# In every second weight chunk, a DMA adds the weights onto their negated high part to form the low part

## The chip, the cores and the metric

The kernel runs on one core of one Trainium2 chip. The metric is the device time of one execution in microseconds (us). Before the change the median of three runs is 1270.47 us (1269.8 to 1270.65).

## What is computed

The reference is a two-layer encoder over 256 tokens of width 2048, in fp32. Cut to what matters:

```python
# layer 0: differential attention (A) and spatial gating (B) from one input product
proj = rms_norm(x, g0) @ w_in            # 2048 x (4*2048 + 3*2048)
q, k, v, z_a, u_b, v_b, z_b = split(proj)
y_a = head_norm(diff_attention(q, k, v)) * silu(z_a)
y_b = spatial_gating(gelu(u_b), gelu(v_b)) * silu(z_b)
x = x + concat(y_a, y_b) @ w_out
# layer 1: a gated linear recurrence
xb, z_c = split(rms_norm(x, g1) @ w_in1)  # 2048 x (2*2688)
h = rg_lru(causal_conv4(xb))              # two block-diagonal gate products and a scan
x = x + (h * silu(z_c)) @ w_out1
return rms_norm(x, gf)
```

Nearly all the arithmetic is products of 256 tokens with some 229 MB of weights, each of which is used once.

## The kernel before

**Weights.** The weights are laid out in the order of their use as 228 chunks of up to 16 tiles of 128 x 128 (`plan()`): the chunks vb, u, zb, q, k, v, ob, za and oa of layer 0 (chunks 0 to 143), then the loop of layer 1 with its xb, zc and gt chunks (144 to 206), then the output product co (207 to 227). A full chunk is 128 x 2048 fp32, 1 MiB. The gate chunks gt are smaller, 4 to 8 tiles, and 21 of the 63 chunks of layer 1's loop are such.

**Products in parts.** The products run in a rounded fp32 format (F32R). To keep precision each operand is split into a high part (the value rounded to that format) and a low part (the rest, w minus its high part), and three of the four partial products are taken: high x high, high x low, low x high. So every chunk needs two SBUF tiles before TensorE can use it: `hi` and `lo`. `feat` (L264) and `tokn` (L280) hold the products; in each tile the product with `hi` comes first and the one with `lo` behind it.

**The walk.** `run` (L235) does one chunk per step. In step s TensorE does the products of chunk s, while the split of chunk s + 2 (`LA` = 2) and the load of chunk s + 5 (`LD` = 5) are recorded. `load` (L174) issues one DMA on SP's queue into a `raw` tile, of which there are three. `split_hi` (L192) is a ScalarE copy from `raw` to `hi`, `split_lo` (L207) a VectorE subtraction `lo = raw - hi`. `hi` and `lo` have three buffers each as well, so the buffer for chunk s + 2 is the one that chunk s - 1 used: the ScalarE copy of step s can start when TensorE is through with chunk s - 1, that is, at the moment when step s begins on TensorE. A `raw` buffer is free when the last reader of the chunk in it is through, and SP's DMA for the chunk three later waits for that. Chunks 0 to 5 (below `FINE` = 6) are loaded and split in quarters and aren't touched by the change.

**Order.** The order on each engine is written out by hand (`manual_schedule`): within a step come the work of phase -1 (evacuations of the products before), the split's ScalarE part, the work of phase 0, the split's VectorE part, the loads, the work of phase 1, the products, and the work of phase 2. All engines run their instructions in that order.

Of the kernel before, what the change touches and what calls it, by code (L numbers as in the profile page):

```python
# [11 lines left out]
AF = mybir.ActivationFunctionType  # L12
# [16 lines left out]
NEG = -3.0e38  # L29
# how far the recurrent branch's input product runs ahead of its gates  # L30
LEAD = 3
# the shift of the sigmoid that starts the reciprocal
SHIFT = 8.0

# columns of the packed per-feature parameters
PRM = {}
# [9 lines left out]
def gate_rows(j):  # L46
    """The 128-feature tiles that share a gate block with tile j."""
    heads = lambda t: set(range(t * P // CB, (t * P + P - 1) // CB + 1))
    return [k for k in range(KC) if heads(k) & heads(j)]


def z_rows(j):
    """The gate path's column tiles by the recurrent branch's tile j: at first the same, one behind later."""
    return range(j, j + 1) if j < KC // 2 else range(j - 1, j - (j == KC // 2))


def plan():
    """The weights' tiles in the order of their use: chunks of up to 16 tiles of 128 x 128."""
    chunks = []
    add = lambda kind, **kw: chunks.append(dict(kind=kind, **kw))  # L60
    for cb in range(4):
        for kq in range(4):
            add("vb", cb=cb, kq=kq, n=16)
    for ct in range(KD):
        add("u", ct=ct, n=16)
        add("zb", ct=ct, n=16)

    def heads(p):
        for h in (2 * p, 2 * p + 1):
            for j in range(2):  # L70
                add("q", h=h, j=j, n=16)
            for j in range(2):
                add("k", h=h, j=j, n=16)
        for kq in range(4):
            add("v", p=p, kq=kq, n=16)

    def za(p):
        for kq in range(4):
            add("za", p=p, kq=kq, n=16)

    def out(kind, rows, wait):
        """An output product; the first column tiles leave the row tiles from wait[1] on for later."""
        cols, late = wait
        order = [(f, k) for f in range(cols) for k in range(late)]
        order += [(f, k) for f in range(cols) for k in range(late, rows)]
        order += [(f, k) for f in range(cols, KD) for k in range(rows)]
        for t in range(0, len(order), 16):
            add(kind, fk=order[t:t + 16], n=len(order[t:t + 16]))

    heads(0)  # L90
    for f in range(KD):
        add("ob", f=f, n=16)
    za(0)
    for p in range(1, H // 2):
        heads(p)
        za(p)
    out("oa", KD, (4, KD - 4))
    for j in range(LEAD):
        add("xb", j=j, n=16)
    for j in range(KC):  # L100
        if j + LEAD < KC:
            add("xb", j=j + LEAD, n=16)
        for z in z_rows(j):
            add("zc", j=z, n=16)
        add("gt", j=j, n=2 * len(gate_rows(j)))
    add("zc", j=KC - 1, n=16)
    out("co", KC, (4, KD))
    off = 0
    for c in chunks:
        c["off"] = off  # L110
        off += c["n"] * P * P
    return chunks, off
# [3 lines left out]
def trunk(ctx, tc, xT, prm, rep, wsp, wst, out):  # L116
# [10 lines left out]

# [1 line left out]
    pt = cpool.tile([P, NPRM], F32, name="pt")  # L129
# [18 lines left out]

    # an operand's two parts lie side by side, tile by tile
    class Parts:  # L150
# [15 lines left out]

# [1 line left out]
    chunks, _ = plan()  # L168
# [5 lines left out]
    def load(c):  # L174
# [6 lines left out]
        for a in range(4):  # L181
# [3 lines left out]
            SP.dma_start(t[:, a * 512:a * 512 + 512], src[:, a * 512:a * 512 + 512])  # L185

    def split_x(k):
        A.activation(x.hi[k], res[:, k, :], AF.Copy, scale=par("g0", k))
        V.scalar_tensor_tensor(x.lo[k], res[:, k, :], par("g0", k), x.hi[k].bitcast(F32),
                               op0=ALU.mult, op1=ALU.subtract)  # L190

    def split_hi(c):  # L192
# [4 lines left out]
        if c >= FINE:  # L197
            A.copy(hi[:, :n], raw[c][:, :n])  # L198
            return
        for a in range(4):  # L200
# [6 lines left out]
    def split_lo(c):  # L207
        n = chunks[c]["n"] * P
        hi, lo = parts[c]
        if c >= FINE:  # L210
            V.tensor_sub(lo[:, :n], raw[c][:, :n], hi[:, :n].bitcast(F32))  # L211
        del raw[c]

    # the tensor engine's clock rises while the first loads are under way
    warm = pst.tile([P, 512], F32, tag="o", name="warm")
    for _ in range(10):
        T.matmul(warm[:, :P], ones, ones, start=True, stop=True)

# [1 line left out]
    def at(s, fn, ph=0):  # L220
        """Something due at step s: -1 before the coming chunk's first part, 0 and 1 before and after its second,
        2 after the products."""
        assert (s, ph) > passed[0], (s, ph)
        todo.setdefault((s, ph), []).append(fn)

    def due(s, ph):
        passed[0] = s, ph
        # what yields goes on by turns, so that an operation's wait for the one before it is used
        chains = [c for c in [fn() for fn in todo.pop((s, ph), [])] if isinstance(c, GeneratorType)]
# [5 lines left out]
    def run(emit):  # L235
        """One chunk: later ones' loads and splits, its products, and what is due."""
        s = pos[0]
# [24 lines left out]

# [1 line left out]
    def feat(ps, hi, lo, tiles, m, first, last, whole=False):  # L264
        """W.T x, feature by token, in two halves of ps that are yet to be added, or whole in the first:
        tiles = (tile of the chunk, row tile)."""
        for n, (w, k) in enumerate(tiles):
# [12 lines left out]
    def tokn(pss, hi, lo, kq, first, last):  # L280
        """pss[t][token, n] += x.T W, four row tiles of W, 512 columns."""
        for k in range(4):
# [11 lines left out]
    def halves(out, ps):  # L294
        """The sum of the two halves: ScalarE brings one, before the step's other work."""
        assert passed[0][1] == -1
# [5 lines left out]

# [1 line left out]
    def r_sum(more=()):  # L304
        """Per token 1 / rms, from the sums of squares in acc (and more)."""
        ps = pst.tile([P, 512], F32, tag="t", name="ps_r")
# [17 lines left out]
    def norm_at(s):  # L324
        """The norm's steps from s on; rb is there from step s + 3 on."""
        box = []
# [18 lines left out]

# [1 line left out]
    state = {}  # L347
# [7 lines left out]
    def token_chunks(name):  # L355
        """x.T W of the coming four chunks, 512 columns: a tile for each half of the tokens."""
        pss = [mm_tile(f"ps_{name}_{t}") for t in range(NT)]
# [8 lines left out]
    def do_heads(p):  # L366
        """The first two's tiles pass through pools that open only after step `start` where p is 0."""
        first = pos[0]
# [29 lines left out]

    # ======================= layer 0, the gated spans =======================
    with tc.tile_pool(name="pb", bufs=2) as pb:  # L400
# [7 lines left out]

        # the squares pass through the room of v
        sq = vx.rearrange("p t d -> p (t d)")  # L410
# [126 lines left out]

    # ======================= layer 0, attention =======================
    def lam_dots():
# [9 lines left out]
    def softplus():  # L549
        """4 softplus(-lambda) and -8 of it, softplus as max(-lambda, 0) + log1p(exp(-|lambda|)), log1p by 2 atanh(y / (2 + y))."""  # L550
        lam = par("lam", 0, KC)
# [17 lines left out]
    with tc.tile_pool(name="pa", bufs=2) as pa:  # L569
# [131 lines left out]

        # the gated spans' half of the output product stands in yh, yl until its last tile is through
        at(pos[0], lam_dots, 2)
# [7 lines left out]

# [1 line left out]
        def x1_add(f, ps):  # L713
# [8 lines left out]
        def out_product(kind, rows, done):  # L722
            """The chunks of an output product; done(f, ps, step) when a column tile is through."""
            cur = {}
# [20 lines left out]

    # ======================= layer 1 =======================
    with tc.tile_pool(name="pc", bufs=2) as pc:
# [45 lines left out]

        # with v = 4 softplus(-lambda) r: a = exp(-2 v) = q - 1, 1 - a^2 = tanh(v) q^2 and q = 2 / (1 + tanh(v)),
        # q by a Newton step from a sigmoid's tail
        def gates(j, ps):
# [101 lines left out]

# [1 line left out]
        last = []  # L900
# [22 lines left out]
def pack(np, i):  # L923
    """The inputs laid out as the program reads them."""
    w0, wo0, w1, wo1 = i["ab_w_in"][0], i["ab_w_out"][0], i["c_w_in"][0], i["c_w_out"][0]
# [84 lines left out]
```

## Time and profile before

| | |
|---|---|
| median of the runs | 1270.47 us |
| the profiled execution's own span | 1268.5 us |
| busy TensorE (PE) | 1256.2 us, 99% of the span |
| busy VectorE (DVE) | 837.2 us, 66% |
| busy ScalarE (ACT) | 641.4 us, 51% |
| busy GpSimd (POOL) | 81.7 us, 6% |
| DMA, mean over the span | 184 GB/s |

The profile is of one execution, whose span lies 2.0 us under the median. The rows below are of four kinds: the page's groups of instructions (count, busy time and mean of one), lists of waits (who waited for whom, total us, times, longest), time lines of one engine over a few steps, and tables of stretches with the busy time of each engine, the granted TensorE clock (1.00 is the full 2.4 GHz) and the share of time in which the 16 DMA engines were busy.

### The profile page before, as it was taken

To read this page: it belongs to the slowest core of one execution; us is meant where nothing else is said; L and a number is where in the kernel's file an instruction comes from. 1 tells how busy PE (TensorE), PEld (TensorE's weight loads), DVE (VectorE), ACT (ScalarE), POOL (GpSimd) and SP (SyncE) were. 2 spreads that over 40 slices of the span, in tenths; PEclk is the share of its full clock that TensorE was granted. 3 is DMA by queue.
4 is the path that set the end of the run, shared out by engine and by line. 5 is a ranking of instruction groups with operands and counts; after the bars stand their busy time and mean duration, and the time that the engine had idled before them with its cause. 6 is when DMAs were issued, how large, how long until landed. Compare 5 with 4: busy or idle time off the path is not lost.

```text
span 1268.5 us, 18568 instructions
## 1 busy us (share of the span) xinstructions
PE 1256.2 (99%) x7647; PEld 1122.2 (88%) x7647; DVE 837.2 (66%) x1116; ACT 641.4 (51%) x850; POOL 81.7 (6%) x72
## 2 busy tenths in 40 slices
PE   9999999999999999999999999999999999999996
PEld 7888888888888888888888888899999999998886
DVE  6747777776566547547547557667788888886543
ACT  7444444443353344444444344445767776685441
POOL 1100000000000000010010012330000000001331
PEclk9999999999999999999999999999999999999998
DMA  9654545455544554554454454544555555556541
GB/s 332 247 196 171 194 169 200 168 189 176 197 168 148 216 198 167 174 188 169 171 186 175 168 184 180 192 151 161 191 198 177 176 195 176 180 208 209 174 164 67
DMA packets 38533, 233.01 MB, mean 184 GB/s; under 512 B 4400, under 2 KB 5296, under 8 KB 12720
## 3 DMA queue, kind: packets, MB, share of 16 engines
q1 hardware_dynamic: 37296, 229.40, 51.3%
q10 hardware_dynamic: 1152, 2.42, 0.5%
q8 instruction: 60, 0.98, 0.3%
q14 instruction: 25, 0.20, 0.0%
HBM read 229.71 MB, written 2.10 MB: 183 GB/s over the span
## 4 chain that ended last, share of the span: by engine, by line
PE 96%; DVE 1%; issue 1%; DMA 1%; ACT 0%; SPq 0%; POOLq 0%; POOL 0%; DVEq 0%; ACTq 0%
PE ps_co L275 6%; PE ps_ob L275 5%; PE ps_k L275 5%; PE ps_q L275 5%; PE ps_zb L275 5%; PE ps_u L275 5%; PE ps_oa L275 4%; PE ps_xb L271 3%; PE ps_xb L273 3%; PE ps_xb L272 3%; PE ps_co L276 3%; PE ps_zc L273 3%; PE ps_zc L271 3%; PE ps_zc L272 3%; PE ps_u L276 2%; PE ps_q L276 2%
## 5 line engine op out<-in xcount | busy, mean ns | idle before, releaser
L211 DVE TENSOR_TENSOR lo<-raw,hi 128x2048 fp32r<-128x2048 f32 (+2 forms) x222 | 481.9, 2171 | 233.2 <-ACT hi L198 232.8
L198 ACT CAST hi<-raw 128x2048 fp32r<-128x2048 f32 (+2 forms) x222 | 402.4, 1813 | 356.5 <-PE ps_za L290 55.3
L275 PE MATMUL ps_co<-y,hi 128*128 128x512 f32 x315 | 110.2, 399 | 0.0
L273 PE MATMUL ps_zc<-x,lo 128*128 128x256 f32 x336 | 95.3, 284 | 0.2 <-DVE lo L211 0.2
L271 PE MATMUL ps_xb<-x,hi 128*128 128x256 f32 x336 | 95.4, 284 | 0.0
L273 PE MATMUL ps_xb<-x,lo 128*128 128x256 f32 x336 | 95.3, 284 | 0.0
L271 PE MATMUL ps_zc<-x,hi 128*128 128x256 f32 x336 | 95.2, 283 | 0.0
L272 PE MATMUL ps_zc<-x,hi 128*128 128x256 f32 x336 | 95.2, 283 | 0.0
L272 PE MATMUL ps_xb<-x,hi 128*128 128x256 f32 x336 | 95.2, 283 | 0.0
L275 PE MATMUL ps_zb<-x,hi 128*128 128x512 f32 x256 | 91.7, 399 | 0.0
L275 PE MATMUL ps_q<-x,hi 128*128 128x512 f32 x256 | 91.3, 399 | 0.0
L275 PE MATMUL ps_k<-x,hi 128*128 128x512 f32 x256 | 91.0, 399 | 0.0
L275 PE MATMUL ps_u<-x,hi 128*128 128x512 f32 x256 | 90.6, 393 | 0.0
L275 PE MATMUL ps_ob<-y,hi 128*128 128x512 f32 x256 | 90.5, 400 | 0.0
L276 PE MATMUL ps_co<-y,lo 128*128 128x256 f32 x315 | 86.0, 281 | 0.0
L275 PE MATMUL ps_oa<-y,hi 128*128 128x512 f32 x240 | 83.8, 399 | 0.0
L275 PEld LDWEIGHTS ps_co<-y,hi 128*128 128x128 f32 x315 | 58.4, 188 | 13.2
L276 PE MATMUL ps_q<-x,lo 128*128 128x256 f32 x256 | 69.2, 281 | 0.0
L276 PE MATMUL ps_ob<-y,lo 128*128 128x256 f32 x256 | 69.2, 281 | 0.0
L276 PE MATMUL ps_u<-x,lo 128*128 128x256 f32 x256 | 69.2, 281 | 0.0
L276 PE MATMUL ps_k<-x,lo 128*128 128x256 f32 x256 | 69.2, 280 | 0.0
L276 PE MATMUL ps_zb<-x,lo 128*128 128x256 f32 x256 | 68.5, 278 | 0.0
(288 smaller groups left out, 2854.6 us busy)
## 6 DMA issues: line engine op xcount, KB each, us to landing
raw<-in_wst SPq DMA_DIRECT2D x201, 1024.0 KB, 4.8
raw<-in_wst SPq DMA_DIRECT2D x26, 256.0 KB, 6.0
raw<-in_wst SPq DMA_DIRECT2D x11, 384.0 KB, 3.1
raw<-in_wst SPq DMA_DIRECT2D x8, 512.0 KB, 4.8
res<-in_xT SPq DMA_DIRECT2D x3, 512.0 KB, 7.2
out_x<-res SPq DMA_DIRECT2D x4, 256.0 KB, 2.3
out_x<-res ACTq DMA_DIRECT2D x3, 256.0 KB, 2.3
res<-in_xT SPq DMA_DIRECT2D x4, 128.0 KB, 3.5
```

The source lines that it names most:

```text
L198: A.copy(hi[:, :n], raw[c][:, :n])
L211: V.tensor_sub(lo[:, :n], raw[c][:, :n], hi[:, :n].bitcast(F32))
L271: T.matmul(ps[:, :S], hi[:, s], m.hi[k], start=a, stop=False)
L272: T.matmul(ps[:, :S], hi[:, s], m.lo[k], start=False, stop=False)
L273: T.matmul(ps[:, :S], lo[:, s], m.hi[k], start=False, stop=b)
L275: both = lambda: T.matmul(ps, hi[:, s], m.both[k], start=a, stop=b)
L276: small = lambda: T.matmul(ps[:, :S], lo[:, s], m.hi[k], start=False, stop=False)
```

## The change

In every chunk of even number from 6 on, the VectorE subtraction is gone. ScalarE writes the negated, rounded weights into `lo` right after it has written `hi`, and a DMA issued on GpSimd's queue then reads the chunk's weights from HBM again and adds them onto what stands in `lo`. Of the 222 chunks from 6 on these are 111. The chunk's own load into `raw` stays, since ScalarE reads it twice.

```diff
+    def by_dma(c):
+
+        return c >= FINE and c % 2 == 0
+
...
         if c >= FINE:
             A.copy(hi[:, :n], raw[c][:, :n])
+            if by_dma(c):
+                A.activation(lo[:, :n], raw[c][:, :n], AF.Copy, scale=-1.0)
+                src = wst[chunks[c]["off"]:chunks[c]["off"] + P * n].rearrange("(p c) -> p c", p=P)
+                GP.dma_start(lo[:, :n], src, accum_op=ALU.add)
             return
...
     def split_lo(c):
         n = chunks[c]["n"] * P
         hi, lo = parts[c]
-        if c >= FINE:
+        if c >= FINE and not by_dma(c):
             V.tensor_sub(lo[:, :n], raw[c][:, :n], hi[:, :n].bitcast(F32))
         del raw[c]
```

The rest of the diff takes out comments, so line numbers of the changed kernel differ by up to 8.

ScalarE's order in the ob chunks of layer 0, before (`hi`, `raw` and `lo` are a chunk's tiles, the numbers tell buffers apart, `l_y` is a small vector for layer 1):

```order
L198 CAST hi_3291<-raw_3167 128x2048
L554 ACTIVATE l_y<-pt 128x21
L555 ACTIVATE l_y<-l_y 128x21
L198 CAST hi_3356<-raw_3215 128x2048
L198 CAST hi_3397<-raw_3256 128x2048
L198 CAST hi_3438<-raw_3321 128x2048
```

And the same place in the changed kernel:

```order
L202 CAST hi_3323<-raw_3198 128x2048
L204 ACTIVATE lo_3324<-raw_3198 128x2048
L562 ACTIVATE l_y<-pt 128x21
L563 ACTIVATE l_y<-l_y 128x21
L202 CAST hi_3389<-raw_3247 128x2048
L202 CAST hi_3430<-raw_3288 128x2048
L204 ACTIVATE lo_3431<-raw_3288 128x2048
```

Every second copy into `hi` has an instruction that writes `lo` behind it, ahead of the step's other ScalarE work.

GpSimd's order from the start of layer 0 to its first attention heads, before (`rt`, `sd` and `ss` are the small vectors of the norms, raised to the power -1/2):

```order
L416 TENSOR_TENSOR vx<-vx 128x1024 x3
L316 TENSOR_TENSOR rt<-rt,mhalf 128x2
L469 TENSOR_TENSOR sd<-sd,mhalf 128x2
L639 TENSOR_TENSOR ss_3152<-ss_3152,mhalf 128x2
L639 TENSOR_TENSOR ss_3158<-ss_3158,mhalf 128x2
```

And in the changed kernel around the last two of these:

```order
L206 DMA lo_3010<-in_wst 128x2048
L206 DMA lo_3128<-in_wst 128x2048
L647 TENSOR_TENSOR ss_3183<-ss_3183,mhalf 128x2
L647 TENSOR_TENSOR ss_3189<-ss_3189,mhalf 128x2
L206 DMA lo_3234<-in_wst 128x2048
L206 DMA lo_3324<-in_wst 128x2048
```

GpSimd's queue, which held nothing between those vectors, now holds one DMA for each two chunks.

## Rows read from the trace of the kernel before

**Rows 1.** The page: busy us, share of the span, instructions of each engine.
```profile
PE 1256.2 (99%) x7647; PEld 1122.2 (88%) x7647; DVE 837.2 (66%) x1116; ACT 641.4 (51%) x850; POOL 81.7 (6%) x72
```

**Rows 2.** The list of waits of TensorE: total us, times, longest.
```profile
PE warm L217 <- DVE ones L138: 1.1, 1, 1.1
...
PE ps_vb L289 <- DVE lo L205: 0.4, 2, 0.2
PE ps_zc L273 <- DVE lo L211: 0.2, 1, 0.2
```

**Rows 3.** The page's chain that ended last: shares of the span by engine.
```profile
PE 96%; DVE 1%; issue 1%; DMA 1%; ACT 0%; SPq 0%; POOLq 0%; POOL 0%; DVEq 0%; ACTq 0%
```

**Rows 4.** The page's groups of the split: count | busy, mean ns | idle before.
```profile
L211 DVE TENSOR_TENSOR lo<-raw,hi 128x2048 fp32r<-128x2048 f32 (+2 forms) x222 | 481.9, 2171 | 233.2 <-ACT hi L198 232.8
L198 ACT CAST hi<-raw 128x2048 fp32r<-128x2048 f32 (+2 forms) x222 | 402.4, 1813 | 356.5 <-PE ps_za L290 55.3
```

**Rows 5.** ScalarE's time line in the ob chunks: start, us, [idle before].
```profile
406.14 1.91 ACT L198 CAST hi<-raw 128x2048 fp32r<-128x2048 f32 x1 [3.37 <-PE ps_ob L275]
411.79 1.91 ACT L198 CAST hi<-raw 128x2048 fp32r<-128x2048 f32 x1 [3.74 <-PE ps_ob L275]
417.44 1.91 ACT L198 CAST hi<-raw 128x2048 fp32r<-128x2048 f32 x1 [3.74 <-PE ps_ob L275]
```

**Rows 6.** ScalarE's groups by form: copying with a scale, and as a cast.
```profile
L803 ACT ACTIVATE q<-q 128x256 f32<-128x256 f32 x21 | 8.8, 418 | 0.7
L835 ACT CAST y<-zz 128x256 fp32r<-128x256 f32 x21 | 8.5, 404 | 11.4 <-DVE zz L832 11.4
```

**Rows 7.** GpSimd's groups by form.
```profile
L340 POOL TENSOR_TENSOR acc<-acc,sqr 128x256 f32<-128x256 f32 x29 | 53.2, 1833 | 93.1 <-ACT sqr L333 92.7
L639 POOL TENSOR_TENSOR ss<-ss,mhalf 128x2 f32<-128x2 f32 x8 | 11.6, 1444 | 620.6 <-DVE ss L638 345.7 <-PE ps_o L630 274.9
L316 POOL TENSOR_TENSOR rt<-rt,mhalf 128x2 f32<-128x2 f32 x3 | 2.1, 705 | 18.3 <-DVE rt L315 18.3
```

**Rows 8.** The tile raw, 380 to 440 us: the ten loads, us from issue to landing.
```profile
L179 SPq DMA_DIRECT2D raw<-in_wst x10: 327/328/328, 388.2 to 438.7; - x10
...
DMA to landing us min/median/max: 4.6/4.7/5.4
```

**Rows 9.** The loads' line L179 over the whole span.
```profile
L179 SPq DMA_DIRECT2D raw<-in_wst x222: 327/328/328, 25.0 to 1226.0; - x111
...
DMA to landing us min/median/max: 2.6/4.8/8.0
```

**Rows 10.** Stretches: length, PE, PEld, DVE, ACT, POOL busy, clock, DMA share, GB/s.
```profile
100.00:790.00 690.00, 690.00 (x3751) 596.12 (x3750) 436.79 (x568) 302.75 (x390) 18.24 (x14) 1.00 0.51 180
790.00:1130.00 340.00, 340.00 (x2712) 333.51 (x2711) 263.19 (x393) 220.29 (x320) 24.05 (x33) 1.00 0.52 180
```

**Rows 11.** VectorE's and SP's time lines in the ob chunks: a subtraction, the next load.
```profile
413.73 2.29 DVE L211 TENSOR_TENSOR lo<-raw,hi 128x2048 fp32r<-128x2048 f32 x1 [0.53 <-ACT hi L198]
...
416.05 0.33 SPq L179 DMA_DIRECT2D raw<-in_wst  x1
```

**Rows 12.** ScalarE's time line over three steps of layer 1's loop.
```profile
901.19 1.91 ACT L198 CAST hi<-raw 128x2048 fp32r<-128x2048 f32 x1 [3.05 <-PE ps_zc L272]
...
903.62 1.04 ACT L198 CAST hi<-raw 128x1024 fp32r<-128x1024 f32 x1
...
909.08 1.90 ACT L198 CAST hi<-raw 128x2048 fp32r<-128x2048 f32 x1 [2.20 <-PE ps_xb L272]
...
914.84 1.91 ACT L198 CAST hi<-raw 128x2048 fp32r<-128x2048 f32 x1 [0.70 <-PE ps_zc L272]
```

## The prediction

> **What bounds the kernel now.** I read the page's busy times first: TensorE is busy 99% of the span, VectorE 66%, ScalarE 51%, GpSimd 6% [rows 1]. The reader is to see that only TensorE is near its limit. TensorE's list of waits says the same from the other side: nothing that it waits for costs more than 1.1 us in all, and the subtraction that the change removes kept it waiting once, for 0.2 us [rows 2]. The chain that ended last is 96% TensorE and 1% VectorE [rows 3]. So time taken off VectorE can bring next to nothing, and the question is whether the new way of making `lo` is still in time for TensorE. For that I read the time line of ScalarE over whole steps, then the loads' times to landing, then the share of time in which the DMA engines are busy.
>
> A step of layer 0 is 5.65 us long: ScalarE's copies into `hi` begin at 406.14, 411.79 and 417.44, each at once behind the last product of the step before, which frees the buffer [rows 5]. In layer 1's loop three steps, one of them a small gate chunk, take 914.84 - 901.19 = 13.65 us [rows 12], so two steps take 9.1 us on the average, and two of which one is a gate chunk 909.08 - 901.19 = 7.9 us.
>
> **What goes.** 111 VectorE subtractions of 2.17 us [rows 4], 241 us of VectorE's 837. They lie beside TensorE's products and aren't on the path: gain 0 to 0.2 us [rows 2].
>
> **What comes, on ScalarE.** 111 instructions of the size of the copy, 1.91 us each [rows 5]; that a copy with a scale costs what a cast costs is seen in the small ones, 418 and 404 ns [rows 6]. That is 111 x 1.81 = 201 us (mean with the small chunks [rows 4]), ScalarE's 641 become 842 of 1268. In layer 1's loop, where it is busiest, 220 of 340 us [rows 10], the new work there is some 60 us. It stays covered by the products: nothing by itself. If that cover were gone, one late copy would cost TensorE at most its own 1.9 us.
>
> **What comes, as a chain.** Now `lo` of an even chunk c is ready only at the end of this: the end of chunk c - 3 on TensorE, copy into `hi` (1.9), negated copy into `lo` (1.9), issue on GpSimd, landing. TensorE needs it at the start of chunk c, two steps behind the chain's start, plus some 0.3 us, since a product with `hi` comes first. With 0.1 us between engines the ScalarE part is H = 3.9 us for a full chunk. So the DMA has 11.3 + 0.3 - 3.9 = 7.7 us from the negated copy's end in layer 0, and in layer 1 across a gate chunk 7.9 + 0.3 - 3.9 = 4.3 us.
>
> The DMA's length L has these parts:
> - GpSimd's issue. No row shows a DMA issued there. SP's issue takes 0.33 us [rows 8], GpSimd's small operations 0.7 to 1.8 us [rows 7]. I take 1.1, bounds 0.3 and 1.8.
> - What a load has beside the bytes. A full load lands 4.7 us after its issue where loads are mostly alone [rows 8]. From 100 to 790 us the engines moved 180 GB/s in 0.51 of the time [rows 10], 353 GB/s while busy, so 1.05 MB occupy all of them for 2.97 us. The rest, 4.7 - 3.0 = 1.7 us, is fixed.
> - The bytes. To add, a DMA has to read the weights from HBM and `lo` from SBUF, so twice what a load reads: 2 x 2.97 = 5.9 us. No row shows such a DMA; the nearest is a load, which puts the lower bound at 2.97, and the upper is open: I take 4 x 2.97 = 11.9 for it.
> - Company. The negated copy is the last reader of `raw` in an even chunk, so its end also releases SP's next load, as the subtraction's end does now (413.73 + 2.29 = 416.02, issue at 416.05 [rows 11]). Both transfers start together and share the engines: + 2.97 us. That loads get in each other's way is seen in their range, 2.6 to 8.0 us [rows 9].
>
> So L = 1.1 + 1.7 + 3 x 2.97 = 11.7 us for a full chunk, 4.0 us over what layer 0 leaves.
>
> On the issue alone, the Trainium skill (DMA: Bandwidth & Descriptors, Specifications) gives about 1 us to the first byte from GpSimd against 0.6 from SP, so 0.4 us more than a load; as an estimate by that page L would be 0.7 us shorter and the sum 39 us less. On the bytes it says (Collectives: The Full Stack, The bandwidth ceiling: the fold count and why AG ≠ RS ≠ AR) that a DMA that adds is slowed by its two source reads, not by the addition, at 32.35 against 62.28 GB/s; no row here shows that, and by it the sum would be that of twice a load's bytes.
>
> **The sum.** If the chain is too long by e, TensorE waits e before chunk c. The next even chunk's chain begins at the end of chunk c - 1, ahead of that wait, so it has e more room, and the waits settle at e/2 for each pair of chunks.
> - Layer 0 and the last output product hold 69 + 10 = 79 even chunks: e = 3.9 + 11.7 - 11.3 - 0.3 = 4.0, so 2.0 x 79 = 158 us.
> - Layer 1's loop holds 32. Their mean size is 0.81 of a full chunk (gate chunks have 4 to 8 of 16 tiles), so H = 3.2 and L = 2.8 + 0.81 x 8.9 = 10.0: e = 3.2 + 10.0 - 9.1 - 0.3 = 3.8, so 1.9 x 32 = 61 us.
>
> Together 219 us: the profiled execution of 1268.5 us would become 1487.5, and with the 2.0 us by which the median lies above it, **1490 us**. The engines would be busy 651 us for the loads (0.51 of the span) and 111 x 0.94 x 5.94 = 620 us for the additions, 85% of that time, so they can carry it, with little to spare.
>
> GpSimd's own queue is no obstacle: its operations wait for VectorE or ScalarE work of the same step, and last 0.7 to 1.8 us [rows 7]. In the sixteen steps of each norm's squares they may hold up a DMA by 1.8 us; that is in the issue's bound.
>
> **The rivals.**
> - *The addition costs what a load costs.* Shared, L = 1.1 + 1.7 + 2 x 2.97 = 8.7 (layer 1: 7.6): e = 1.0 and 1.4, so 0.5 x 79 + 0.7 x 32 = 62 us, 1332 us. Alone, L = 5.8: layer 0 is in time, and the two in three of layer 1's 32 that lie across a gate chunk are late by 5.8 - 4.3 = 1.5, 21 x 1.5 = 32 us, 1302 us. For it: the engines are half idle now [rows 10]. Against it: `lo` must be read as well. Chance 22%, 1295 to 1400 with the cases between.
> - *Twice a load*, the forecast: 1400 to 1570, with the issue's bounds (0.7 us up or down are 39 us) and less or more company. Chance 45%.
> - *The addition is slower than its reads*, three times a load's bytes or more: L = 14.7, layer 1 12.4: e = 7.0 and 6.2, so 277 + 99 = 376 us, 1646 us; four times, 1800 us. The waits are then 3 to 7 us long. The granted clock is 1.00 in both stretches [rows 10], where TensorE never stops; at its lower level of 1.2 GHz a product would take up to twice as long, and no row here shows how such waits affect it. Against it: nothing in a load's rows makes the engines slow. Chance 28%, half of it over 1700.
> - *It ends on the other side, not slower.* The chain is in time even across a gate chunk: that needs L of 4.3 us or less, which is under a load's 4.7 without any issue. It decides from there: 1270 us, or 1268 if VectorE's relief shortens the few waits of [rows 2] and those around layer 1's last scans. Chance 5%, one of it faster by over 0.2%.
>
> **How the numbers follow.** Forecast 45%, load-priced 22%, slower addition 28%, no change 4%, faster 1%. The range leaves out the 5% at the bottom and the 14% above 1700: 1295 to 1700 us. A difference of 0.2% (2.5 us) is about what a measurement of this kernel can tell from none: faster 0.01, same 0.04, slower 0.95.
>
> **What would show it.** In the changed kernel's profile TensorE's list of waits should name the DMA into `lo`, some 220 us in all, for nearly all even chunks and no odd ones; VectorE's waits cost nothing. The DMA's own row should give some 10 us from issue to landing for 1024 KB, and its queue about twice the busy share for each byte that the loads' queue has. The granted clock should stay near 1.00. ScalarE's group that writes `lo` should read 111 times, 1.8 us. The prediction is wrong in its size if the landing is under 8 or over 14 us; in its mechanism if TensorE waits for ScalarE, or for loads of `raw` that the additions pushed back; and wholly if TensorE waits for nothing new.

## The result: slower by a quarter, and the profile after

The changed kernel takes 1594.32 us (median of 4 runs, 1590.56 to 1600.57) against 1270.13 us before, a ratio of 1.2555 (95% interval 1.2523 to 1.2588). That is slower, as forecast, and inside the range of 1295 to 1700 us, but 324 us more and not the 220 of the sum. The profiled execution has a span of 1598.8 us.

The page's busy times of the changed kernel (us, share of the span, instructions), to be held against [rows 1]:

```profile
PE 1366.2 (85%) x7647; PEld 1201.3 (75%) x7647; DVE 600.6 (38%) x1005; ACT 831.1 (52%) x961; POOL 164.7 (10%) x183
...
PEclk9899899999999898898898899998899999989998
```

Two things are to be seen. TensorE's span has 1598.8 - 1366.2 = 232.6 us in which it does nothing; before, 12.3. And the same 7647 matmuls keep it busy for 110 us longer, 1366.2 against 1256.2, because the granted clock, second row, is below full in many slices; its mean over the span is 0.912, before 0.996. These two parts, 220 and 110 us, are the whole difference of 330 us between the spans.

TensorE's list of waits (who waited for whom: us in total, times, longest), which answers to [rows 2]:

```profile
PE ps_zc L281 <- DMA lo<-in_wst: 68.9, 12, 8.0
PE ps_u L284 <- DMA lo<-in_wst: 32.1, 9, 6.3
PE ps_q L284 <- DMA lo<-in_wst: 21.2, 6, 4.7
PE ps_co L284 <- DMA lo<-in_wst: 18.6, 6, 4.4
PE ps_v L297 <- DMA lo<-in_wst: 16.9, 4, 4.9
PE ps_za L297 <- DMA lo<-in_wst: 14.6, 4, 4.4
PE ps_oa L284 <- DMA lo<-in_wst: 13.2, 4, 3.9
PE ps_vb L297 <- DMA lo<-in_wst: 13.0, 4, 7.8
PE ps_ob L284 <- DMA lo<-in_wst: 9.6, 4, 4.0
PE ps_k L284 <- DMA lo<-in_wst: 7.2, 2, 4.0
PE ps_xb L281 <- DMA lo<-in_wst: 4.9, 3, 3.6
```

All eleven rows name the new DMA, and they add up to 220.2 us in 58 waits of 3.8 us. The page's rows on the DMAs show how long an addition takes. First the queues (packets, MB, share of 16 engines' span), then the issues by line (KB each, us to landing):

```profile
q1 hardware_dynamic: 37296, 229.40, 43.2%
q0 software_dynamic: 15984, 111.03, 35.2%
...
raw<-in_wst SPq DMA_DIRECT2D x201, 1024.0 KB, 5.9
lo<-in_wst POOLq DMA_DIRECT2D x102, 1024.0 KB, 11.1
```

The additions (q0) took 0.352 x 1598.8 = 563 us of all engines for 111.03 MB, 5.3 us per 1.05 MB; the loads (q1) 691 us for 229.40 MB, 3.2 us. An addition lands 11.1 us after its issue begins.

One chain can be read off whole in the ob chunks. ScalarE's time line, then GpSimd's and TensorE's at the same place (start, us, [idle before]):

```profile
476.76 1.91 ACT L202 CAST hi<-raw 128x2048 fp32r<-128x2048 f32 x1 [4.30 <-PE ps_ob L283]
478.58 1.91 ACT L204 ACTIVATE lo<-raw 128x2048 fp32r<-128x2048 f32 x1
...
487.98 1.90 ACT L202 CAST hi<-raw 128x2048 fp32r<-128x2048 f32 x1 [3.74 <-PE ps_ob L283]
489.78 1.90 ACT L204 ACTIVATE lo<-raw 128x2048 fp32r<-128x2048 f32 x1
...
504.47 1.91 ACT L202 CAST hi<-raw 128x2048 fp32r<-128x2048 f32 x1 [3.65 <-PE ps_ob L283]
```

```profile
480.78 0.90 POOL L206 DMA_DIRECT2D lo<-in_wst  x1 [7.35 <-ACT lo L204]
491.98 0.86 POOL L206 DMA_DIRECT2D lo<-in_wst  x1 [10.30 <-ACT l_y L562]
```

```profile
491.84 0.58 PE L284 MATMUL ps_ob<-y,lo 128*128 128x256 f32 x1 [3.67 <-DMA lo<-in_wst]
492.22 0.63 PE L283 MATMUL ps_ob<-y,hi 128*128 128x512 f32 x1
```

The chain starts at 476.76, the addition is issued at 480.78 and lands 11.06 us later, at 491.84, where TensorE has waited 3.67 us for it. The next chain started at 487.98, before that wait ended; its addition, issued at 491.98, is there by about 503.0 if it takes as long. TensorE is through with the two chunks in between only at 504.47, where ScalarE's last copy shown begins, so that addition isn't waited for. The products behind the wait are slow: 0.58 us for 256 columns and 0.63 for 512, where 0.28 and 0.40 are usual. The stretches before, behind and after show why (as in [rows 10], the third number from the end is the granted clock):

```profile
480.00:491.80 11.80, 8.17 (x47) 6.78 (x45) 3.13 (x3) 6.21 (x5) 0.90 (x1) 0.99 0.86 226
491.80:495.00 3.20, 3.16 (x10) 2.77 (x11) 2.50 (x15) 0.22 (x1) 0.86 (x1) 0.50 1.01 330
495.00:503.00 8.00, 8.00 (x47) 7.03 (x47) 4.37 (x10) 1.91 (x1) 0.00 (x0) 1.00 0.85 189
```

Up to the end of the wait the clock is full, in the 3.2 us behind it 0.50, the lower level of 1.2 GHz, and then full again.

### The profile page after: what moved, and what is told of

Read it like the earlier page. It is cut to its first block, busy times and chain, and to the rows that moved or that the text cites. A ratio compares the mean times of both kernels' runs of the same rounds, so it can differ in the third digit from the quotient of the medians.

```text
span 1598.8 us, 18805 instructions
## 1 busy us (share of the span) xinstructions
PE 1366.2 (85%) x7647; PEld 1201.3 (75%) x7647; DVE 600.6 (38%) x1005; ACT 831.1 (52%) x961; POOL 164.7 (10%) x183
## 3 DMA queue, kind: packets, MB, share of 16 engines
q1 hardware_dynamic: 37296, 229.40, 43.2%
q0 software_dynamic: 15984, 111.03, 35.2%
## 4 chain that ended last, share of the span: by engine, by line
PE 44%; DMA 33%; issue 17%; ACT 4%; DVE 1%; POOL 1%; SPq 0%; POOLq 0%; DVEq 0%; ACTq 0%
DMA lo<-in_wst 32%; PE ps_q L283 3%; PE ps_u L283 2%; PE ps_co L283 2%; ACT lo L204 2%; PE ps_zc L281 2%; PE ps_zc L279 2%; PE ps_zc L280 2%; PE ps_zb L283 2%; PE ps_q L284 2%; PE ps_ob L283 2%; PE ps_oa L283 2%; PE ps_xb L281 2%; PE ps_xb L279 1%; PE ps_xb L280 1%
## 5 line engine op out<-in xcount | busy, mean ns | idle before, releaser
L219 DVE TENSOR_TENSOR lo<-raw,hi 128x2048 fp32r<-128x2048 f32 (+2 forms) x111 | 238.6, 2149 | 230.8 <-ACT hi L202 230.6
L206 POOL DMA_DIRECT2D lo<-in_wst x111 | 96.8, 872 | 1256.8 <-ACT lo L204 776.0
L204 ACT ACTIVATE lo<-raw 128x2048 fp32r<-128x2048 f32 (+2 forms) x111 | 203.1, 1830 | 0.0
L281 PE MATMUL ps_zc<-x,lo 128*128 128x256 f32 x336 | 107.9, 321 | 68.9 <-DMA lo<-in_wst 68.9
L281 PEld LDWEIGHTS ps_zc<-x,lo 128*128 128x128 f32 x336 | 75.6, 225 | 71.4 <-DMA lo<-in_wst 71.4
L279 PE MATMUL ps_zc<-x,hi 128*128 128x256 f32 x336 | 105.3, 313 | 0.0
L283 PE MATMUL ps_u<-x,hi 128*128 128x512 f32 x256 | 105.3, 440 | 0.0
L284 PE MATMUL ps_u<-x,lo 128*128 128x256 f32 x256 | 77.4, 313 | 32.1 <-DMA lo<-in_wst 32.1
L280 PE MATMUL ps_zc<-x,hi 128*128 128x256 f32 x336 | 104.8, 312 | 0.0
L283 PE MATMUL ps_q<-x,hi 128*128 128x512 f32 x256 | 102.1, 433 | 0.0
L284 PEld LDWEIGHTS ps_u<-x,lo 128*128 128x128 f32 x256 | 56.1, 219 | 37.1 <-DMA lo<-in_wst 36.1
## 6 DMA issues: line engine op xcount, KB each, us to landing
lo<-in_wst POOLq DMA_DIRECT2D x102, 1024.0 KB, 11.1
```

The costliest lines, as they stand in the source:

```text
L204: A.activation(lo[:, :n], raw[c][:, :n], AF.Copy, scale=-1.0)
L206: GP.dma_start(lo[:, :n], src, accum_op=ALU.add)
L279: T.matmul(ps[:, :S], hi[:, s], m.hi[k], start=a, stop=False)
L280: T.matmul(ps[:, :S], hi[:, s], m.lo[k], start=False, stop=False)
L281: T.matmul(ps[:, :S], lo[:, s], m.hi[k], start=False, stop=b)
L283: both = lambda: T.matmul(ps, hi[:, s], m.both[k], start=a, stop=b)
```

## The experiments

Two theories of the 220 us were set against each other. By the **chain theory** TensorE waits because copy, negated copy, issue and landing are together longer than two steps. By the **capacity theory** the DMA engines (busy 79% of the span) are the bound, and nothing but fewer bytes helps. For the 110 us, a **clock theory**: the clock falls after waits of some 4 us, not from load or traffic. In the diffs the changed kernel is the old side.

### Negated copy first

```diff
-            A.copy(hi[:, :n], raw[c][:, :n])
             if by_dma(c):
                 ...
                 GP.dma_start(lo[:, :n], src, accum_op=ALU.add)
+            A.copy(hi[:, :n], raw[c][:, :n])
```

> The changed kernel with ScalarE's two instructions in even chunks exchanged: the negated copy into lo goes first, the copy into hi behind it, so the DMA that adds is issued 1.9 us earlier in each chain and nothing else differs. Chain theory (TensorE waits because copy + negated copy + issue + landing is longer than two steps): the waits for lo, 220 us in the changed kernel, fall by 1.9 / 2 x 111 = 105 us to about 115 us. Clock addition (the 110 us by which TensorE's busy time grew, 1366 against 1256 us, come from waits of about 4 us each): with waits of about 2 us the clock stays near 1.00 and the time is about 1385 us; if the clock falls all the same, 1440 to 1490. Capacity theory (the DMA engines, busy 79% of the span, are the bound and an earlier start brings nothing): no change, 1560 to 1600 us.

Measured: 1362.09 us, ratio to before 1.0723 (1.0702 to 1.0745). Exchanging two instructions takes back 232 of the 324 us, which the capacity theory doesn't allow. TensorE waited 67 us for `lo` (43 times, 1.6 us on the average), less than the 115 expected, since the landing fell too:

```profile
raw<-in_wst SPq DMA_DIRECT2D x201, 1024.0 KB, 7.9
lo<-in_wst POOLq DMA_DIRECT2D x102, 1024.0 KB, 9.2
```

The addition lands in 9.2 us and the load now takes 7.9 (changed kernel: 11.1 and 5.9). Here the copy into `hi`, not the negated one, is the last to read `raw`, so the load starts 1.9 us behind the addition and no longer together with it. That head start is worth 1.9 us of the addition's landing; the two transfers still overlap behind it, so this isn't all that the company costs. The granted clock is 0.982, and the time is 23 us under the 1385 expected.

### Products with lo last

```diff
-            both = lambda: T.matmul(ps, hi[:, s], m.both[k], start=a, stop=b)
-            small = lambda: T.matmul(ps[:, :S], lo[:, s], m.hi[k], start=False, stop=False)
-            for f in (small, both) if b else (both, small):
-                f()
...
+        for n, (w, k) in enumerate(tiles):
+            if not end(n):
+                T.matmul(ps, hi[:, s(w)], m.both[k], start=first and n == 0, stop=False)
+        for n, (w, k) in enumerate(tiles):
+            T.matmul(ps[:, :S], lo[:, s(w)], m.hi[k], start=False, stop=False)
```

The same is done for the sums that are taken whole, in `tokn` and in the output products; a sum's last product with `hi` stays at its end.

> The changed kernel with the products of a chunk in another order: all products with hi first, then all with lo (the gate chunks stay as they are). The DMAs, ScalarE and the number of products don't change; TensorE needs lo some 3.4 us later in a chunk. Chain theory: the lateness of 3.8 us falls to about 0.4, so waits of 10 to 40 us in all, the clock back near 1.00, 1285 to 1320 us. Capacity theory: the engines have the same bytes to move, so the wait only shows at another product: 1540 to 1600 us.

Measured: 1386.22 us, 1.0913 (1.088 to 1.0947): most of the loss goes with the same DMAs, which speaks for the chain, but 66 us above the expectation. 52 waits remain, 76 us, and TensorE's busy time is 1286.3 us, 30 above the kernel before. The landing didn't fall; the first row has the DMA engines' busy tenths in 40 slices of the span:

```profile
DMA  8998999999989999989999999888899888889993
...
lo<-in_wst POOLq DMA_DIRECT2D x102, 1024.0 KB, 11.6
```

The same bytes had to go in less time, and the engines were busy nine tenths or more in most slices. So capacity isn't the bound, but it probably feeds back into the landing; no run tells that apart.

### Both

> Both: the negated copy first and the products with lo last, 5.3 us of room together against a lateness of 3.8. Chain theory: no waits for lo but perhaps a few us at gate chunks, clock 1.00, within 0.5% of the kernel before, 1268 to 1277 us, with the DMA engines over 90% busy. Capacity theory: the additions and loads together are 1260 us of engine time in the changed kernel, so they would hold the kernel at 1350 us or more.

Measured: 1297.64 us, 1.0222 (1.0197 to 1.0247), a miss by 21 us in the direction of the capacity theory, though far from its 1350. TensorE's waits:

```profile
PE ps_zc L280 <- DMA lo<-in_wst: 10.8, 6, 4.3
PE ps_xb L280 <- DMA lo<-in_wst: 6.8, 7, 1.7
PE ps_rb L334 <- POOL rt L329: 3.5, 2, 2.5
PE ps_vb L303 <- DMA lo<-in_wst: 2.4, 1, 2.4
```

The waits for `lo` are in layer 1's loop (zc, xb, and 1.0 us in a gate chunk), where gate chunks shorten the room, and once in the start-up (vb). In the chunks between there is none.

### The same where the room is full

```diff
-        return c >= FINE and c % 2 == 0
+        return 16 <= c < 144 and c % 2 == 0
```

(On top of both edits.)

> The kernel with the negated copy first and the products with lo last, and with the addition by DMA only in the even chunks 16 to 142, that is in layer 0 behind its start: 64 additions, none where gate chunks shorten the room. Chain theory: the chain is in time in every one of them, no waits for lo, 1268 to 1274 us. Capacity theory (loads and additions together fill the DMA engines to 99% while both run, so additions are late whatever their room): over half of what the kernel with both edits and all 111 additions lost, 1285 us or more.

Measured: 1265.95 us, 0.9974 (0.9964 to 0.9983), no wait for `lo` at all. Its row for 100 to 780 us (length, busy PE, PEld, DVE, ACT, POOL, clock, DMA share, GB/s):

```profile
100.00:780.00 680.00, 679.87 (x3710) 591.77 (x3709) 297.15 (x502) 403.24 (x443) 64.02 (x70) 1.00 0.93 270
```

The DMA engines are 93% busy at 270 GB/s, TensorE doesn't stop, the clock is 1.00. With this the capacity theory falls as a bound: the engines carry the loads and every second chunk's addition at TensorE's full pace, if each has its time.

### The order of the products by itself

The control for the three kernels above: their order of products, no addition by DMA.

> The kernel without any addition by DMA and with the products with lo last: the control for the runs that have that order. Expected: the order by itself changes nothing, 1268 to 1274 us. If it costs something, that is to be taken from the other runs' losses.

Measured: 1264.84 us, 0.996 (0.9944 to 0.9976). The order isn't neutral, it gains 5 us, so against this control the kernel with both edits lost 33 us (21 of waits for `lo`, 9 of TensorE's busy time), and the one with additions in layer 0 alone 1 us. ScalarE's copies, which follow TensorE's steps, show the gain in the ob chunks:

```profile
411.17 1.92 ACT L202 CAST hi<-raw 128x2048 fp32r<-128x2048 f32 x1 [3.65 <-PE ps_ob L289]
416.73 1.91 ACT L202 CAST hi<-raw 128x2048 fp32r<-128x2048 f32 x1 [3.65 <-PE ps_ob L289]
```

A step is 5.56 us, where [rows 5] have 5.65. That matmuls of 512 and 256 columns take turns isn't enough to explain it. In the u chunks of the kernel before they take turns just so, and a step is 5.56 us all the same:

```profile
236.67 1.92 ACT L198 CAST hi<-raw 128x2048 fp32r<-128x2048 f32 x1
...
242.23 1.92 ACT L198 CAST hi<-raw 128x2048 fp32r<-128x2048 f32 x1
```

By tile, TensorE's busy time falls by 0.9 us each in q, k and ob, 1.1 in oa and 1.5 in co, which is 5.3 of 5.5 us in all, and not in u and zb. What sets these chunks apart is open. This kernel is 0.4% faster than the one before, clear of its interval, and it needs no DMA for that.

### Half as many additions

```diff
-        return c >= FINE and c % 2 == 0
+        return c >= FINE and c % 4 == 2
```

> The changed kernel with the DMA that adds in every fourth chunk only (55 in place of 111), the subtraction on VectorE in all others. Chain theory: a chain that follows a wait has that much more room, which is why in the changed kernel only every second addition is waited for (58 waits of 3.8 us); every fourth chunk's chain has no wait before it, so all 55 are waited for, each some 3.5 to 4 us: about 200 us of waits, the clock as in the changed kernel, 1530 to 1600 us. Capacity theory: half the added bytes, so at most half of the loss, 1270 to 1430 us.

Measured: 1556.23 us, 1.2252 (1.2227 to 1.2276). Half the additions (56 by the page's count), and 88% of the loss is still there, as the chain theory alone says. TensorE waited 201 us, 52 times, 3.9 us on the average; the first rows:

```profile
PE ps_zc L281 <- DMA lo<-in_wst: 40.9, 6, 8.3
PE ps_xb L281 <- DMA lo<-in_wst: 36.8, 6, 8.4
PE ps_u L284 <- DMA lo<-in_wst: 28.7, 8, 4.7
```

The DMA engines' share falls back to five to seven tenths in most slices, and an addition still lands in 10.8 us. A wait in front of chunk c gives chunk c + 2's chain as much more room, so in the changed kernel's layer 0 every second addition was free; here the free ones are left out.

### Work in the place of waits

```diff
+    def fill(ps, w, v):
+        if by_dma(pos[0]):
+            for _ in range(17 if v.shape[-1] == S else 9):
+                T.matmul(ps, w, v, start=True, stop=True)
```

(Called ahead of the first product of a sum, where a chunk begins one.)

> The changed kernel with useless products put in front of the first product that reads lo, in 91 of the 111 even chunks: the chunk's first product with hi is done 9 times more (17 times where it has half the columns), some 2.05 us of TensorE's time each, 187 us in all; the sum is then started anew, so the result doesn't change. Chain theory: a chain has 2 us more room at its start and 2 us at its end, so where TensorE waited 3.8 us before every second even chunk it now works 2 us in each of them, and fillers and remaining waits together take what the waits took, 220 to 240 us. Clock theory (the other 110 us of the changed kernel are a lower clock that follows waits of 3 to 5 us): with the long waits gone the clock is back near 0.99 and the kernel is faster for 187 us of extra work, 1490 to 1530 us. Rival (the clock falls for another reason, the load on the chip or the DMA traffic): the same 0.91 and 1590 to 1620 us.

Measured: 1562.89 us, 1.2306 (1.227 to 1.2342), 31 us less than the changed kernel although TensorE does 1075 useless matmuls more. Its rows of the page and its clock:

```profile
PE 1474.0 (94%) x8722; PEld 1304.6 (84%) x8722; DVE 601.5 (39%) x1005; ACT 831.2 (53%) x961; POOL 164.6 (11%) x183
...
PEclk9899999999999999999999999999999999999989
```

The mean clock is 0.979, and 74 us of waits remain. The extra busy time is 1474.0 - 1256.2 = 218 us: some 187 of fillers, by the expectation's estimate, which leaves 31 for the clock, where the changed kernel lost 110 to it. So the clock part of the expectation held, with the DMA traffic almost as before. The time is 33 us over its range because fillers and waits took 187 + 74 = 261 us and not 220 to 240: the changed kernel waited before 58 chunks only, so some of the 91 fillers probably stood where there was little or no wait to replace.

### A DMA that only writes

```diff
-                GP.dma_start(lo[:, :n], src, accum_op=ALU.add)
+                GP.dma_start(lo[:, :n], src)
```

> The changed kernel with a DMA that only writes the weights into lo, in place of one that adds them; lo then holds the weights themselves, so the result leaves out the low part of every even chunk. It tells what the reading of lo costs. Chain theory with two reads: a packet takes what a load's takes (309 ns for 8 KB against 628), the landing falls from 11.1 to about 8 us, the lateness from 3.8 to under 1, waits of 20 to 70 us, 1290 to 1345 us. Rival (what costs is the issue on GpSimd's queue or the format's conversion, which this DMA has too): landing near 11 us and 1550 us or more.

Measured: 1359.13 us, 1.0702 (1.067 to 1.0733). Queue and landing:

```profile
q0 software_dynamic: 15984, 111.03, 20.9%
...
lo<-in_wst POOLq DMA_DIRECT2D x102, 1024.0 KB, 7.1
```

0.209 x 1358.0 = 284 us for the same 111.03 MB, where the addition took 563: adding costs twice the engine time of writing, 5.3 against 2.7 us per 1.05 MB. The landing is 7.1 us and not 11.1. The waits are 59 us, as expected; the time is 14 us over the expectation's upper end, since the clock still fell to 0.977 and TensorE's busy time grew by 29 us.

### Half of each addition

```diff
-                A.activation(lo[:, :n], raw[c][:, :n], AF.Copy, scale=-1.0)
+                h = n // 2
+                A.activation(lo[:, :h], raw[c][:, :h], AF.Copy, scale=-1.0)
...
-                GP.dma_start(lo[:, :n], src, accum_op=ALU.add)
+                GP.dma_start(lo[:, :h], src[:, :h], accum_op=ALU.add)
...
+            h = n // 2 if by_dma(c) else 0
+            V.tensor_sub(lo[:, h:n], raw[c][:, h:n], hi[:, h:n].bitcast(F32))
```

> The changed kernel with the addition, and the negated copy, for the first half of each even chunk's columns only; VectorE subtracts the other half. Chain theory: 1 us less on ScalarE and half of the addition's 5.9 us of bytes, landing about 8 us: the chain is in time in layer 0 (lateness 0 or less) and late by under 2 us across gate chunks, 1272 to 1300 us. Capacity theory (loss in proportion to the added bytes): half of 324 us, about 1430 us.

Measured: 1365.57 us, 1.0752 (1.0721 to 1.0783), outside both expectations. The landing is as expected:

```profile
PE ps_zc L283 <- DMA lo<-in_wst: 31.8, 11, 5.1
PE ps_co L286 <- DMA lo<-in_wst: 7.4, 5, 3.3
PE ps_vb L299 <- DMA lo<-in_wst: 5.5, 2, 5.2
...
lo<-in_wst POOLq DMA_DIRECT2D x102, 512.0 KB, 8.3
```

TensorE waited 62 us, half of it in zc chunks; layer 0's chunks behind vb have 12 us together in its list, so there the chain is about in time, as the theory says. What was wrong is my figure for the gate chunks: by the theory's own terms, 7.9 + 0.3 - 2.9 = 5.3 us of room against a landing of 8.3 is 3.0 us of lateness, not under 2, and the measured waits in zc are 2.9 us on the average. The other 34 us are the clock (0.975; TensorE busy 1290.1 us), which the expectation left out.

### ScalarE's new work alone

```diff
-                src = wst[chunks[c]["off"]:chunks[c]["off"] + P * n].rearrange("(p c) -> p c", p=P)
-                GP.dma_start(lo[:, :n], src, accum_op=ALU.add)
...
-        if c >= FINE and not by_dma(c):
+        if c >= FINE:
```

> The changed kernel without its DMA: ScalarE still writes the negated copy into lo, and VectorE then makes lo by subtraction in every chunk, as before. It prices ScalarE's new work by itself. Expected by the sum: nothing, 1268 to 1274 us. Rival (ScalarE's 203 us more push back evacuations and copies): over 1280 us.

Measured: 1276.68 us, 1.0052 (1.0032 to 1.0071): a loss of 7 us where none was expected. TensorE now waits for VectorE's subtraction, which comes later by the negated copy ahead of it:

```profile
PE ps_zc L279 <- DVE lo L217: 3.7, 2, 2.2
...
PE ps_xb L279 <- DVE lo L217: 0.8, 2, 0.4
```

These rows are 4.5 us, all in layer 1's loop, and TensorE's busy time is 2 us up. In the changed kernel VectorE has less to do, and its TensorE waits for ScalarE as little as before (0.9 us in both lists), so 7 us should be the most that ScalarE's part costs there; no run shows that part by itself.

## Why the prediction was right, and where it was short

**VectorE's relief brings nothing.** Right: TensorE was the bound, and no row of after shows a gain.

**The chain, its length and the room.** Right, and shown from three sides: 1.9 us less at its start takes back 232 us, 3.4 us more at its end 208 us, and half the additions almost nothing. The terms of L came out as follows.

| term | taken | measured |
|---|---|---|
| GpSimd's issue | 1.1 us | 0.87 us (mean of the 111 issues) |
| an addition's bytes | twice a load's, 5.9 us | 5.3 us per 1.05 MB, twice a write's 2.7; the loads beside it 3.2 |
| company of the load | 3.0 us | not by itself: 11.1 - 0.9 - 1.7 - 5.3 leaves 3.2 us if the fixed part is a load's 1.7 |
| L for a full chunk | 11.7 us | 11.1 us from issue to landing |

```profile
L206 POOL DMA_DIRECT2D lo<-in_wst x111 | 96.8, 872 | 1256.8 <-ACT lo L204 776.0 <-ACT y L540 219.7 <-ACT y L843 110.9
```

That the addition costs twice a transfer without it decided between an end at 1302 to 1332 us and one at 1646 and over. The Trainium skill (Collectives: The Full Stack, The bandwidth ceiling: the fold count and why AG ≠ RS ≠ AR) puts such a factor down to the add's two source reads, and has its figures from a reduce-scatter against an all-gather, 32.35 against 62.28 GB/s. The runs here agree with the factor, 563 against 284 us of engine time for the same bytes; that a second read is the cause no run here shows. The addition's cost is not only engine time, since the room for it is counted from issue to landing.

**The waits.** 219 us were forecast and 220 measured, a closer match than the method deserves. Layer 0 and the last output product have 146 us where the sum had 158, layer 1's loop has 74 where it had 61. L was 0.6 us shorter than taken, and the start-up, which the sum treats like the rest, has a wait of 7.8 us. The text expected waits before nearly all even chunks, at half the lateness. They came before fewer, at the whole of it. In layer 0 that is every second even chunk, most at 3 to 5 us. In layer 1's loop it is mostly every third, and there they are the longest, as at this zc chunk:

```profile
1309.53 0.58 PE L281 MATMUL ps_zc<-x,lo 128*128 128x256 f32 x1 [6.66 <-DMA lo<-in_wst]
```

The two steps ahead of such a chunk hold a gate chunk. The prediction's own room for that case, 4.3 us, against a landing of 11.1 gives 6.8 us, and six waits in a row are 6.5 to 7.2. The sum had used the loop's mean room of 9.1 us for every chunk instead (and the mean size of all 63 chunks, 0.81, where the 32 even ones have 0.84, some 6 us). So the total is right in part by luck, and the waits were longer than those it was made of, which matters for the next point.

**The clock.** This is the step that failed. The prediction said that the granted clock should stay near 1.00 and had no term for it; it told of waits of 3 to 7 us and the lower level only among the rivals. The 1.00 that it went by [rows 10] was read where TensorE never stops. Measured is 0.912, and 110 us, a third of the loss. With these the time is 1594 us, above the 1400 to 1570 of the forecast's own case; that it lies in the range at all is owed to the range's upper part, which was drawn for an addition slower than its reads, and the addition wasn't that. Over the runs:

| kernel | waits for lo, us | times | mean, us | clock |
|---|---|---|---|---|
| changed kernel | 220 | 58 | 3.8 | 0.912 |
| half as many additions | 201 | 52 | 3.9 | 0.927 |
| half of each addition | 62 | 38 | 1.6 | 0.975 |
| DMA that only writes | 59 | 30 | 2.0 | 0.977 |
| products with lo last | 76 | 52 | 1.5 | 0.978 |
| filler | 74 | 34 | 2.2 | 0.979 |
| negated copy first | 67 | 43 | 1.6 | 0.982 |
| both | 21 | 15 | 1.4 | 0.992 |
| additions in layer 0 alone | 0 | 0 | | 0.996 |

The filler run has the changed kernel's DMAs and a busier TensorE and still a clock of 0.979, so neither the traffic nor TensorE's load lowers it; the waits do. The run with additions in layer 0 says the same of the traffic: with the DMA engines 93% busy and no wait the clock is 1.00. The means hide single waits of 3 to 9 us in every run of the table that has waits. How long a wait may be before the clock falls no run was made to find.

**The rivals.** A load-priced addition fell with the DMA that only writes, whose engine time is half; that its waits are 59 us, near the rival's 62, is chance, since 36 of them are in layer 1's loop, where the rival had 22, and the clock comes on top. The slower addition fell with 5.3 us per 1.05 MB, less than twice a load's. Not slower fell by 324 us. That the engines can carry the traffic, which the sum put at 85% of the time, is shown up to 93% by the run with additions in layer 0.

**ScalarE's new work.** Put at nothing; it is 7 us where VectorE still subtracts, and in the changed kernel it wasn't measured by itself.

## What to carry to other kernels

A new producer is judged by its whole chain, from the event that frees its buffer to the first reader, against the room between these two, and in the stretch where the room is shortest; the share of busy time of the engines on it says little. Before an engine that is the bound is made to wait, look for where the chain can start earlier or its reader come later: here one exchange of two instructions was worth 232 us, and a later reader together with it all but 28 us of the loss. A long wait of TensorE costs more than its length, since the granted clock falls behind it: here 220 us of waits cost another 110.

## What was not expected of the hardware

- A wait gives the next chain room, so in layer 0 the waits came before every second even chunk and not before each; halving the number of additions left the waits at 201 of 220 us.
- With the clock granted at its lower level after a wait, useless matmuls in the place of waits made the kernel 31 us faster.
- The same matmuls, 512 and 256 columns wide, take 5.56 us for an ob chunk in two groups and 5.65 us in turns, while u chunks take 5.56 us in turns as well; the cause is open. For the whole kernel the two groups are 1264.84 against 1269.99 us, and with 64 of the additions by DMA on top 1265.95 us. That order is the version to keep; of the change itself no form that was run is faster than the control with the same order.
